# A two-layer decoder step: order of loads and constants at the start, and a last down projection by two token groups

## The chip, the cores and the metric

The kernel runs on one core of one Trainium2 chip. The metric is the device time of one execution in microseconds. The engines named below: PE is the tensor engine (matrix products and transposes, into PSUM), PEld its weight loads, ACT the scalar engine (activation functions, copies, casts), DVE the vector engine, POOL the GpSimd engine, SP the sync engine, which issues most of the transfers. Each engine executes its own queue in order. L12 is line 12 of the kernel before.

## The reference, cut to what matters

One inference step of a decoder of two layers with D_MODEL 1024, for a prompt of 1024 tokens and for 8 sample tokens. Layer 0 mixes by a gated linear recurrence beside attention into 256 memory tokens, layer 1 by stick-breaking attention beside memory attention. Each is followed by a SwiGLU network with 2816 middle columns. What stands at the two ends of the kernel:

```python
def rmsnorm(x, g):
    xf = x.astype(jnp.float32)
    y = xf * lax.rsqrt(jnp.mean(xf * xf, axis=-1, keepdims=True) + EPS)
    return (y * g.astype(jnp.float32)).astype(x.dtype)

def swiglu(h, w_gu, w_down):
    gate, up = jnp.split(h @ w_gu, 2, axis=-1)
    return (jax.nn.silu(gate) * up) @ w_down
...
    for l in range(DEPTH):
        g = g_norm[l]
        hn = rmsnorm(h, g[0])
        if l < N_A:
            mix, S = a_mixer(hn, w_in_a[l], lbs[l], hg_norm[l], mem_k[l], mem_v[l], w_o[l], hg_s0[l])
        else:
            mix = b_mixer(hn, w_in_b[l - N_A], sb_bias[l - N_A], k_all, v_all, q_pos, k_pos, mem_k[l], mem_v[l], w_o[l])
        h = h + rmsnorm(mix, g[1])
        h = h + rmsnorm(swiglu(rmsnorm(h, g[2]), w_gu[l], w_down[l]), g[3])
```

The head of the kernel is the first `rmsnorm` and the product with `w_in_a`; the tail is the last `@ w_down`, its `rmsnorm` and the last sum, for the second half of the prompt and the sample tokens.

## The kernel before, in words

**Layout.** Activations lie with features on the 128 partitions and tokens along the free dimension: a tensor of 1024 features is eight blocks of 128. Tokens go in two groups: group 0 has prompt tokens 0 to 511, group 1 has 512 to 1023 and the 8 sample tokens behind them (520 columns). To keep fp32 accuracy, each operand of a product is split in two fp32r parts, x = hi + lo; a product is three matmuls (w_hi x_hi, w_hi x_lo, w_lo x_hi). A block of weights (four 128x128 tiles, 256 KB) is loaded by SP (L261), cast to its hi part on ACT (L266) and subtracted to its lo part on DVE (L267). Group 1's 520 columns go as two matmuls of 260.

**Order.** The code is written in generators that yield after each piece and are woven together. The kernel language's scheduler then lays out each engine's queue before the run: it goes by the order in which the code issues the instructions, and lets an instruction go ahead of an earlier one where, by its own estimate of times, the earlier one isn't ready yet. It also places the waits and gives out the buffers of a pool (`bufs` of them under one tag). `tc.issue_after(ins)` forces what is issued inside it behind `ins` on that engine.

**Head** (L125 to L216, then `start(0, x0)`, L402). Loads of the norm gains and other parameters into `prow` (L128 to L131), then the four token tiles of group 0 (L134, 128 tokens x 1024 each, 512 KB) on SP. A hint for ACT's table of functions (L135). Constants: the identity, `flip`, `trif`, `bound`, `sel`, and `mask`: for 7 levels and 2 sides two selections on POOL (L169, L173) and a cast to bytes on DVE (L177). `prow` is transposed on PE (L182) into `par`, from which the gains are read. Then the lower bound of the recurrence (L197 to L202), a broadcast of the attention offset (L205, L208) and the page table (L211 to L216). `start(0)` norms the four token tiles: `rms_rows` (L391) takes the sum of squares on ACT (L397, tiles 0 and 2) or on DVE (L395, tiles 1 and 3), Ln and Exp on ACT (L398, L399), and scales the tile on DVE (L400). Then, for each of eight feature blocks, four transposes (L425, one for each tile), the hi part with gain on ACT (L428) and the lo part on DVE (L429). The first product is the value projection `rows_proj` (weights L1074, L1076, L1077; 96 matmuls L1082). `flip` is first read behind it (L1099), the masks in the recurrence (L1285).

**Tail** (class `ffn_w`, L644). The last SwiGLU network, group 1 of layer 1, goes in five parts of 5, 5, 4, 4 and 4 middle tiles. Most middle tiles are computed by `gate_up_w` (L553), which ends with two Silu on ACT (L594, L603), products on DVE and the split of the middle tile (L287, L288). Each part then adds its share of the down projection to R (eight tiles of 128 x 520): for each of eight output blocks m, 24 matmuls of 260 columns (L696), an addition for each half on DVE (L705). In the last part, for each block also the square (L339, L342 on ACT), its accumulation over the blocks (L343 on DVE) and a copy scaled by the norm's gain (L708, ACT). After block 3, `first_half` (L763) transposes blocks 0 to 3 back to token rows. After block 7, `finish_rows` (L776) sums the accumulated squares over the features on PE (L782, L783), takes Ln and Exp on ACT, transposes blocks 4 to 7 (L798), and for each of four row tiles and the sample rows computes row * rstd + residual on DVE in two halves (L799, L802) and stores it (L807, L809). The residual rows were made earlier (`token_rows`, `htok`). L688 is a hint to load ACT's table with both Ln and Exp.

Of the kernel before, what the change touches and what calls it, by code (L numbers as in the profile page):

```python
# [9 lines left out]
F32 = mybir.dt.float32  # L10
F32R = mybir.dt.float32r
# [7 lines left out]
P = 128  # L19
# [5 lines left out]
def tile_decoder(  # L25
# [114 lines left out]
    flip = const.tile([P, P], F32, name="flip")  # L140
    nc.gpsimd.affine_select(
        flip, ones, pattern=[[1, P]], compare_op=ALU.is_equal, fill=0.0, base=1 - P, channel_multiplier=1
    )
    epsb = const.tile([P, 1], F32, name="epsb")
    nc.vector.memset(epsb, EPS)
    trif = const.tile([P, P], F32, name="trif")
    nc.gpsimd.affine_select(
        trif, ones, pattern=[[-1, P]], compare_op=ALU.is_ge, fill=0.0, base=0, channel_multiplier=1
    )
    bound = const.tile([P, P], F32, name="bound")  # L150
    nc.vector.memset(bound, TOP)
    nc.gpsimd.affine_select(
        bound, bound, pattern=[[-1, P]], compare_op=ALU.is_gt, fill=-200.0, base=0, channel_multiplier=1
    )
    sel = const.tile([P, NB, NB], F32, name="sel")
    nc.gpsimd.affine_select(
        sel, ones[:, : NB * NB].rearrange("p (b c) -> p b c", c=NB), pattern=[[1, NB], [-1, NB]],
        compare_op=ALU.is_equal, fill=0.0, base=0, channel_multiplier=0,
    )

    mask = const.tile([P, 7, 2, 64], U8, name="mask")
    for lv in range(7):
        m = 1 << lv
        nb = 64 // m
        for side in range(2):
            o = side * m
# [40 lines left out]
    for blk in range(2):  # L207
        nc.vector.tensor_copy(biass[:, blk], biasp.unsqueeze(2).to_broadcast([P, H, NB]))  # L208
# [1454 lines left out]
```

## Time and profile before

| | us |
|---|---|
| median of 3 runs | 2450.96 (2450.86 to 2453.5) |
| the profiled execution's own time | 2454.44 |
| its span in the trace | 2452.7 |
| PE busy | 2413.9 |
| DVE, ACT, POOL busy | 1563.8, 1204.3, 102.6 |

A busy time of PE is matmuls in flight, not PE at its peak. In a row of the chain of waits stand the start, the length, and what the chain goes through: an instruction of an engine by line, a transfer, or "issue". In a row of the timeline: start, length, engine, line, operation, tiles written and read, count, and in brackets how long the engine was idle before it and who released it. In a row of a single line or tile: count, then the shortest, median and longest duration in ns. q, s and ns are PSUM tiles, ws split weights, w raw weights, m middle tiles, r the tiles R, st the accumulated squares, yT output rows.

### The profile page before, as it was taken

How to read it: one execution, taken by the hardware profiler on the slowest of the kernel's cores; microseconds unless marked ns; L12 is line 12 of the kernel's file. 1: busy time of each engine (PE TensorE's matmuls, PEld its weight loads, DVE VectorE, ACT ScalarE, POOL GpSimd, SP SyncE). 2: the span in 40 equal slices, each digit the busy share in tenths (PEclk: the TensorE clock that was granted, in tenths of full speed). 3: DMA queues.
4: the chain of work that ended last, by engine and by line, in shares of the span. 5: the costliest groups of instructions: out<-in, count | busy, mean ns of one | idle time of the engine just before them, and what ended most of it. 6: DMA issues, size and time to landing. Idle time of an engine off the chain costs nothing.

```text
span 2452.7 us, 40619 instructions
## 1 busy us (share of the span) xinstructions
PE 2413.9 (98%) x15473; PEld 2141.9 (87%) x15473; DVE 1563.8 (64%) x2697; ACT 1204.3 (49%) x2354; POOL 102.6 (4%) x153
## 2 busy tenths in 40 slices
PE   7999999999999999999999999999999999999998
PEld 5888988888877887999999989877787898999997
DVE  5777556765775676555544585677677558655665
ACT  4547544444444454555433454555454445564444
POOL 2000000000000000011111100022000000000000
PEclk9999999999999999999999999999999999999998
DMA  5353252263543446686688866453453244375541
GB/s 177 106 157 104 74 159 84 65 178 118 179 136 95 138 146 210 171 221 150 181 201 220 237 187 189 153 163 118 140 154 117 82 126 125 117 200 148 151 134 66
DMA packets 496726, 360.33 MB, mean 147 GB/s; under 512 B 19181, under 2 KB 443738, under 8 KB 496530
## 3 DMA queue, kind: packets, MB, share of 16 engines
q1 hardware_dynamic: 477970, 303.19, 41.2%
q0 software_dynamic: 18560, 54.53, 9.1%
q8 instruction: 122, 2.00, 0.3%
q14 instruction: 74, 0.61, 0.1%
HBM read 327.83 MB, written 75.96 MB: 165 GB/s over the span
## 4 chain that ended last, share of the span: by engine, by line
PE 90%; DVE 4%; DMA 2%; ACT 2%; issue 1%; SPq 0%; POOL 0%; DVEq 0%; ACTq 0%; POOLq 0%
PE mm L280 62%; PE q L581 7%; PE q L696 5%; PE q L539 2%; PE mm L1082 2%; PE s L932 1%; PE s L891 1%; PE s L1265 1%; PE mm L868 1%; PE s L1440 1%; PE mm L841 1%; DMA b<-qd 1%; PE s L1479 1%; PE s L918 1%; DVE ws L267 1%
## 5 line engine op out<-in xcount | busy, mean ns | idle before, releaser
L280 PE MATMUL mm<-x,ws 128*128 128x260 f32 (+1 forms) x7776 | 1330.4, 330 | 0.0
L280 PEld LDWEIGHTS mm<-x,ws 128*128 128x128 f32 x7776 | 1149.2, 188 | 142.9 <-issue 8.2
L266 ACT CAST ws<-w 128x512 fp32r<-128x512 f32 x712 | 420.1, 591 | 685.7 <-PE mm L280 563.6
L267 DVE TENSOR_TENSOR ws<-w,ws 128x512 fp32r<-128x512 f32 x712 | 462.1, 652 | 263.3 <-ACT ws L266 255.7
L280 PE MATMUL mm<-m,ws 128*128 128x512 f32 (+1 forms) x2112 | 393.1, 343 | 0.4 <-DVE r L476 0.4
L280 PEld LDWEIGHTS mm<-m,ws 128*128 128x128 f32 x2112 | 324.3, 189 | 47.3 <-issue 3.4
L696 PE MATMUL q<-m,ws 128*128 128x260 f32 x1056 | 128.8, 283 | 0.0
L696 PEld LDWEIGHTS q<-m,ws 128*128 128x128 f32 x1056 | 127.2, 188 | 0.4 <-ACT hT L514 0.2
L572 DVE TENSOR_TENSOR ws<-w,ws 128x512 fp32r<-128x512 f32 x126 | 86.5, 691 | 59.7 <-ACT ws L571 57.0
L581 PE MATMUL q<-y,ws 128*128 128x260 f32 x864 | 112.9, 283 | 0.0
L571 ACT CAST ws<-w 128x512 fp32r<-128x512 f32 x126 | 78.0, 621 | 67.9 <-PE q L696 27.4
L581 PEld LDWEIGHTS q<-y,ws 128*128 128x128 f32 x864 | 107.6, 188 | 0.0
L476 DVE TENSOR_TENSOR r<-r,mm 128x512 f32<-128x512 f32 (+1 forms) x96 | 66.0, 687 | 59.9 <-PE mm L280 58.8
L320 DVE TENSOR_SCALAR t<-mm 128x512 f32<-128x512 f32 (+1 forms) x74 | 51.2, 692 | 64.3 <-PE mm L280 64.3
L732 DVE TENSOR_TENSOR t<-t,mm 128x512 f32<-128x512 f32 (+1 forms) x66 | 45.5, 689 | 67.9 <-PE mm L280 67.4
L324 DVE TENSOR_TENSOR t<-t,t 128x512 f32<-128x512 f32 (+1 forms) x66 | 45.8, 694 | 65.7 <-ACT t L323 65.7
L581 PE MATMUL q<-x,ws 128*128 128x260 f32 x648 | 86.3, 282 | 0.0
L581 PEld LDWEIGHTS q<-x,ws 128*128 128x128 f32 x648 | 81.3, 188 | 0.0
L343 DVE TENSOR_TENSOR st<-st,n 128x512 f32<-128x512 f32 (+1 forms) x98 | 67.1, 691 | 6.5 <-ACT n L342 5.0
L287 ACT CAST m<-t 128x512 fp32r<-128x512 f32 (+1 forms) x88 | 54.9, 624 | 25.3 <-DVE t L732 16.5
L1018 POOL DMA_INDIRECT c<-in_cache_sb_k,pidx x16 | 16.4, 1026 | 1128.7 <-issue 919.7
L288 DVE TENSOR_TENSOR m<-t,m 128x512 fp32r<-128x512 f32 (+1 forms) x88 | 60.9, 692 | 2.6 <-ACT m L287 1.4
(356 smaller groups left out, 2513.0 us busy)
## 6 DMA issues: line engine op xcount, KB each, us to landing
w<-in_w_gu SPq DMA_DIRECT2D x334, 256.0 KB, 3.1
w<-in_w_down SPq DMA_DIRECT2D x160, 256.0 KB, 2.7
w<-in_w_in_a SPq DMA_DIRECT2D x80, 256.0 KB, 2.9
wsum<-in_w_gu POOLq DMA_DIRECT2D x18, 1024.0 KB, 8.9
w<-wsum SPq DMA_DIRECT2D x72, 256.0 KB, 3.5
w<-in_w_o SPq DMA_DIRECT2D x64, 256.0 KB, 2.7
wsum<-in_w_gu POOLq DMA_DIRECT2D x12, 1280.0 KB, 10.5
w<-in_w_mem_kv SPq DMA_DIRECT2D x32, 256.0 KB, 3.2
```

The costliest lines, as they stand in the source:

```text
L266: nc.scalar.copy(ws[:, 0, :n, :], raw[:, :n, :])
L267: nc.vector.tensor_sub(ws[:, 1, :n, :], raw[:, :n, :], ws[:, 0, :n, :].bitcast(F32))
L280: nc.tensor.matmul(ps[:, a, : PW[g]], wt, xt[k][:, xi, o : o + PW[g]], start=(k == 0 and wi == 0), stop=(k == nk - 1 and wi == 2),)
L287: nc.scalar.copy(dst[0], src)
L288: nc.vector.tensor_sub(dst[1], src, dst[0].bitcast(F32))
L320: nc.vector.tensor_scalar(sv(x, g), pv(ps, g), -44.0, None, op0=ALU.max)
L343: nc.vector.tensor_add(acc[:, :n], acc[:, :n], t[:, :n])
L476: nc.vector.tensor_add(dst, dst, pv(ps, g))
L571: nc.scalar.copy(w[:, 0, :], src)
L572: nc.vector.tensor_sub(w[:, 1, :], src, w[:, 0, :].bitcast(F32))
L581: nc.tensor.matmul(ps[:, :h], w[:, wj, k * P : (k + 1) * P], x[:, xi, :], start=(first and k == 0 and wi == 0), stop=(k == 3 and wi == 2), ...
L696: nc.tensor.matmul(pp[a][:, :h], wt, mids[k][:, xi, a * h : (a + 1) * h], start=(k == 0 and wi == 0), stop=(k == nf - 1 and wi == 2),)
```

## The change

Two places.

**Head.** The four token tile loads are issued ahead of the four parameter loads, and these go through ACT's queue in place of SP's. `flip`, `trif`, `bound`, `sel`, `mask`, the lower bound, the offsets and the page table are written further down in the code, right before `start(0, x0)`; the code that transposes `prow` stays where it was. The cast of the masks goes from DVE to POOL.

```diff
-    prow = tpool.tile([P, P], F32, tag="t", name="prow")
-    nc.vector.memset(prow, 0.0)
-    nc.sync.dma_start(prow[0:NR, :], g_norm.rearrange("l i (k p) -> (l i k) p", p=P))
-    nc.sync.dma_start(prow[NR : NR + ND, :], g_kv.rearrange("(k p) -> k p", p=P))
-    nc.sync.dma_start(prow[NR + ND : NR + ND + H, :], hg_lb.rearrange("l (h p) -> (l h) p", p=P))
-    nc.sync.dma_start(prow[NR + ND + H : NR + ND + H + 1, :], hg_norm)
     xtok = [rpool.tile([P, CH, D], F32, tag="r", name="xtok0")]
     for tb in range(CH):
         nc.sync.dma_start(xtok[0][:, tb, :], x_prompt[0, tb * P : (tb + 1) * P, :])
+    prow = tpool.tile([P, P], F32, tag="t", name="prow")
+    nc.vector.memset(prow, 0.0)
+    nc.scalar.dma_start(prow[0:NR, :], g_norm.rearrange("l i (k p) -> (l i k) p", p=P))
+    nc.scalar.dma_start(prow[NR : NR + ND, :], g_kv.rearrange("(k p) -> k p", p=P))
+    nc.scalar.dma_start(prow[NR + ND : NR + ND + H, :], hg_lb.rearrange("l (h p) -> (l h) p", p=P))
+    nc.scalar.dma_start(prow[NR + ND + H : NR + ND + H + 1, :], hg_norm)
     nc.scalar.preload_act_table_set("natural_log_exp_and_others")
...
-            nc.vector.tensor_copy(mask[:, lv, side, :], mf.rearrange("p b m -> p (b m)"))
...
+            nc.gpsimd.tensor_copy(mask[:, lv, side, :], mf.rearrange("p b m -> p (b m)"))
```

**Tail.** In the last part of `ffn_w` the down projection goes first over columns 256 to 519 (row tiles 2, 3 and the sample rows), then over 0 to 255 (row tiles 0 and 1). The eight split weights are made once and kept for both; three of them take slots of another pool. Each group has its own sums, norm and row operations; those of the first are issued between the blocks of the second. The square of the last block isn't accumulated on DVE; PE adds it in its sums. `first_half` and `finish_rows` are gone. The table hint is forced behind the last Silu.

```diff
-        nc.scalar.activation(sg[:, h:n], gt[:, :h], AF.Silu)
+        done.append(nc.scalar.activation(sg[:, h:n], gt[:, :h], AF.Silu))
...
             if last:
-                self.acc = small([P, WID], tag="st", bufs=3)
-                nc.scalar.preload_act_table_set("natural_log_exp_and_others")
+                with tc.issue_after(done[-1].ins):
+                    nc.scalar.preload_act_table_set("natural_log_exp_and_others")
+                yield from self.down_rows(mids, f0, nf)
+                return
...
+        def down_rows(self, mids, f0, nf):
+            l, n = self.l, NG[1]
+            hT, hsm = htok[0]
+            acc = small([P, WID], tag="st", bufs=3)
+            yt = [xpool.tile([P, D], F32, tag="x0", name=nm("yT")) for _ in range(CH + 1)]
+            ws = []
+
+            def weight(m):
+                raw = wraw.tile([P, 4, P], F32, tag="w", name=nm("w"))
...
+                if m % 3 == 2 or m == 7:
+                    w = cpool.tile([P, 2, 4, P], F32R, tag="c", name=nm("ws"))
+                else:
+                    w = wspl.tile([P, 2, 4, P], F32R, tag="ws", name=nm("ws"))
+                nc.scalar.copy(w[:, 0], raw)
+                nc.vector.tensor_sub(w[:, 1], raw, w[:, 0].bitcast(F32))
+                return w
+
+            def turned(c, k0):
+                o, w = c * P, (P if c < CH else NB)
+                pt = S()
+                for k in range(4):
+                    nc.tensor.transpose(pt[:w, k * P : (k + 1) * P], self.R[k0 + k][:, o : o + w], ident)
+                return pt[:w]
+
+            def front(cs):
+                for c in cs:
+                    w = P if c < CH else NB
+                    nc.scalar.copy(yt[c][:w, :512], turned(c, 0))
+
+            def stats(cs, sq):
+                ps = NS()
+                r = small([P, 8], tag="rr")
+                for i, c in enumerate(cs):
+                    o, w = c * P, (P if c < CH else NB)
+                    nc.tensor.matmul(ps[:w, i : i + 1], acc[:, o : o + w], ones[:, 0:1], start=True, stop=False)
+                    nc.tensor.matmul(ps[:w, i : i + 1], sq[:, o : o + w], ones[:, 0:1], start=False, stop=True)
...
+                for p, i in parts:
+                    nc.scalar.activation(r[p, i], ps[p, i], AF.Ln, scale=1.0 / D, bias=epsb[p])
+                for p, i in parts:
+                    nc.scalar.activation(r[p, i], r[p, i], AF.Exp, scale=-0.5)
+                return r
+
+            def row(c, rc):
...
+                pt = turned(c, 4)
+                nc.vector.scalar_tensor_tensor(
+                    yt[c][:w, :512], yt[c][:w, :512], rc[:w], h[:w, :512], op0=ALU.mult, op1=ALU.add
+                )
+                nc.vector.scalar_tensor_tensor(
+                    yt[c][:w, 512:], pt, rc[:w], h[:w, 512:], op0=ALU.mult, op1=ALU.add
+                )
...
+            late = []
+            for c0, c1, cs in ((256, n, (2, 3, CH)), (0, 256, (0, 1))):
+                for m in range(ND):
+                    if len(ws) <= m:
+                        ws.append(weight(m))
+                    ps = Q(1 + m % 2)[:, : c1 - c0]
+                    for k in range(nf):
+                        for wi, (wj, xi) in enumerate(((0, 0), (0, 1), (1, 0))):
+                            nc.tensor.matmul(
+                                ps, ws[m][:, wj, k, :], mids[k][:, xi, c0:c1],
+                                start=(k == 0 and wi == 0), stop=(k == nf - 1 and wi == 2),
+                            )
+                    if late:
+                        late.pop(0)()
+                    d = self.R[m][:, c0:c1]
+                    nc.vector.tensor_add(d, d, ps)
+                    if m == 0:
+                        nc.scalar.activation(acc[:, c0:c1], d, AF.Square)
+                    else:
+                        sq = N()
+                        nc.scalar.activation(sq[:, c0:c1], d, AF.Square)
+                        if m < ND - 1:
+                            nc.vector.tensor_add(acc[:, c0:c1], acc[:, c0:c1], sq[:, c0:c1])
+                    nc.scalar.activation(d, d, AF.Copy, scale=gcol(l, 3, m))
+                    if m == 4:
+                        front(cs)
...
+                if c0:
+                    it = rest(cs, sq)
+                    late = [lambda: None] + [lambda: next(it)] * (len(cs) + 1)
+                else:
+                    drain(rest(cs, sq))
...
-    drain(f1.part(2), f1.part(3), f1.part(4), f1.finish_rows())
+    drain(f1.part(2), f1.part(3), f1.part(4))
```

`rest` yields `stats` and then one `row` after the other.

More of the change, by code (lines that the diff above doesn't have):

```diff
@@ L745, in part @@
                 self.now = self.R[m][:, 0:1]
-                if last and self.rows:
-                    nc.scalar.activation(
-                        self.R[m][:, :n], self.R[m][:, :n], AF.Copy, scale=gcol(l, 3, m)
-                    )
-                    if m == 3:
-                        first_half(self)
                 if m % 2:
@@ L1570, in store_y @@
             yield
-    x0, x1 = [], []
+    flip = const.tile([P, P], F32, name="flip")
+    nc.gpsimd.affine_select(
+        flip, ones, pattern=[[1, P]], compare_op=ALU.is_equal, fill=0.0, base=1 - P, channel_multiplier=1
+    )
+    trif = const.tile([P, P], F32, name="trif")
+    nc.gpsimd.affine_select(
+        trif, ones, pattern=[[-1, P]], compare_op=ALU.is_ge, fill=0.0, base=0, channel_multiplier=1
+    )
+    bound = const.tile([P, P], F32, name="bound")
+    nc.vector.memset(bound, TOP)
@@ new lines, in tile_decoder @@
+    lb = const.tile([P, H], F32, name="lb")
+    oml = const.tile([P, H], F32, name="oml")
+    lbt = const.tile([P, H], F32, name="lbt")
+    nc.vector.tensor_sub(lbt, lbraw, lbraw)
+    nc.scalar.activation(lbt, lbt, AF.Exp)
+    nc.vector.reciprocal(lb, lbt)
+    nc.vector.tensor_mul(lbt, lbt, lb)
+    nc.vector.tensor_sub(lb, lbt, lbt)
+    nc.vector.tensor_scalar(oml, lb, -1.0, 1.0, op0=ALU.mult, op1=ALU.add)
+    x0, x1 = [], []
+    biasp = const.tile([P, H], F32, name="biasp")
+    nc.sync.dma_start(biasp, sb_bias.rearrange("o h -> (o h)").partition_broadcast(P))
```

163 lines of the change are left out of this document (54 added, 109 removed).

## The prediction

> **What bounds the kernel now.** I read the page first, then busy time by stretch, then the chain of waits at both ends.
>
> ```profile
> span 2452.7 us, 40619 instructions
> ...
> PE 2413.9 (98%) x15473; PEld 2141.9 (87%) x15473; DVE 1563.8 (64%) x2697; ACT 1204.3 (49%) x2354; POOL 102.6 (4%) x153
> ...
> 0.00:20.00 20.00, 4.71 (x18) 3.11 (x18) 10.71 (x36) 8.28 (x20) 14.12 (x41) 1.00 0.55 199
> ...
> 2400.00:2436.40 36.40, 36.39 (x302) 35.81 (x301) 19.09 (x38) 19.83 (x35) 0.00 (x0) 1.00 0.11 33
> 2436.40:2452.70 16.30, 4.85 (x31) 3.26 (x29) 8.14 (x13) 4.62 (x8) 0.00 (x0) 0.62 0.33 131
> ```
>
> The second to last rows give start and end, length, and the busy time of PE, PEld, DVE, ACT and POOL. PE is idle for 2452.7 - 2413.9 = 38.8 us in all: 15.3 of them in the first 20 us, 11.5 after the last projection, and only 12 in the 2400 us between. The change touches the two ends, and removes no matmul. So it can win at most about 27 us, and what it wins is read from the two end chains. The profiled run took 2454.44 us, 1.74 more than its span and 3.5 above the median of 2450.96; I add the differences in the span to the median.
>
> **The head.** The chain of waits from the first token tile to the first product of the value projection (start, length, what):
>
> ```profile
> 3.03 4.87 DMA xtok<-in_x_prompt
> ...
> 7.92 1.23 DVE c L395
> ...
> 13.88 0.42 DVE mask L177 x2
> 14.30 0.15 DVE lb L201
> 14.46 1.25 DVE c L395
> ...
> 15.76 0.30 ACT rr L398
> ...
> 16.08 0.20 ACT rr L399
> 16.28 1.56 ACT ws L1076 x3
> ...
> 17.88 0.76 DVE xtok L400
> ...
> 18.69 0.49 PE ns L425
> ...
> 19.20 0.70 ACT x L428
> ```
>
> The fourth tile's sum of squares (the second L395) starts at 14.46 although its tile is there earlier. Between the two L395, DVE stands in a queue of mask casts, each waiting for POOL's two selections, and of the small lower-bound operations. The first product starts at 19.20 + 0.70 + 0.04 = 19.94.
>
> When is the tile there? One row gives GB/s in slices of 1 us from 0; the other is the next load of SP that had to wait for a token tile's landing:
>
> ```profile
> GB/s 0 0 262 296 218 320 353 315 328 70 186 392 408 418 344 66 8 0 0 0 127 389 203 115 293 241 340 127 170 174 270 401 342 379 337 280 221 283 267 47
> ...
> 10.51 0.33 SPq L820 DMA_DIRECT2D c<-in_mem_prompt  x1
> ```
>
> Slices 2 to 8 sum to 2.09 MB, which is the four tiles of 512 KB: the bytes were moved by 9.0, and the landing was signalled by about 10.4, 1.4 later. Slice 4 has a dip, because tiles 1 to 3 were issued only from 3.03, behind the four parameter loads.
>
> (1) Token tiles first on SP, the parameter loads on ACT's queue. The four issues come 0.45 apart from 0.80. At the 329 GB/s of slices 5 to 8 the 2.1 MB take 6.4 us from 2.0 to 8.4; with the same 1.4 us the last tile lands at 9.8. Bounds: 8.4 (signalled at once) and 10.4 (nothing won). ACT's four issues, less than the 3.03 us in which SP had issued them and the first tile, lie in its wait for the first tile. The weight loads and the two small broadcasts behind the tiles start earlier; they queue behind the same 2.1 MB.
>
> (2) Mask casts from DVE to POOL. DVE then has, behind the last landing, L395, the scaling L400, and perhaps its lower-bound and bias operations (eight of 0.15 to 0.25 us, about 1.3 in all, of which I charge 0.5 as the rest fits into waits for tiles). From 9.8: + 1.25 (L395) + 0.60 (L398 and L399 with their hops, 15.71 to 16.28) + 0.80 (L400) + 0.55 (PE) + 0.74 (L428) + 0.5 = 14.2. Against 19.94 that is **5.7 us**. The 1.56 us of weight casts in the old chain ran while DVE was late and aren't counted. Bounds: tile at 8.4 and no charge gives 12.3, so 7.6; tile at 10.4, the whole 1.3, and 0.7 for a late parameter transpose gives 16.3, so 3.6. After the first product the phase is as before: eight column blocks by the same ACT, DVE and PE work, then PE without a gap.
>
> (3) POOL's longer queue.
>
> ```profile
> L1285 DVE COPY_PREDICATED b<-mask,s x40: 415/451/805, 113.3 to 463.8; 128x256 f32<-128x256 uint8 x40
> ...
> L173 POOL TENSOR_SCALAR_AFFINE_SELECT mf<-mf x14: 234/290/1477, 3.6 to 17.5; 128x64 f32<-128x64 f32 x14
> ```
>
> The numbers behind the count are shortest, median and longest in ns, then the first and last start. POOL's last selections start at 17.5. A u8 cast on POOL has no row; the nearest is L173 with 0.29 on the same shape. Bounds: 0.21 (DVE's own cast, 0.42 for two above) and 1.48 (L173's longest). At 0.29 the 14 casts add 4 us, at 1.48 20.7: done by 22 to 39, while the masks are first read at 113.3. I count nothing; without that cover it would be those 4 us.
>
> **The tail.**
>
> ```profile
> 2410.65 11.55 PE q L696 x96
> 2422.20 1.31 PE q L768 x12
> ...
> 2424.36 0.66 PE q L768 x4
> ...
> 2425.38 0.59 PE q L773 x4
> 2425.97 10.40 PE q L696 x85
> ...
> 2436.40 0.77 DVE r L705 x2
> ...
> 2437.19 0.65 ACT n L342
> ...
> 2437.86 0.71 DVE st L343
> ...
> 2438.61 1.05 PE q L782 x8
> ...
> 2439.87 1.28 ACT L785
> ...
> 2441.17 0.26 ACT rr L785
> ...
> 2441.58 1.28 ACT L786
> ...
> 2443.12 0.75 DVE yT L799
> ...
> 2449.14 0.66 DVE yTs L802
> ...
> 2449.83 0.30 SPq L809 DMA_DIRECT2D out_y_sample<-yTs  x1
> ```
>
> From PE's last product (2436.38) to the end of the span (2452.70) are 16.32 us: a residual add, square, accumulation, the sums on PE, two loads of activation tables, ten row operations of DVE 0.66 apart, and 2.87 for the last store.
>
> (4) Work moved ahead of the last product. The 192 products stay: 96 of 264 and 96 of 256 columns for 192 of 260, 0.120 each. Ahead of the end stood 20 transposes for 1.31 + 0.66 + 0.59 = 2.56, 0.128 each; now there are 32 (12 halves of the first group in front, 12 behind its norm, 8 of the second group), so + 1.54. The first group's sums are 12 instructions, eight as L782 (1.05) and four narrow ones, between nothing and half of that, of which I take 0.28: + 1.33. PE's last product ends 2.87 later, at 2439.25. All else of the first group (six row operations, 4 us of DVE; its scaled copies on ACT) lies beside the second group's 11.5 us of products; the stretch row shows DVE and ACT busy for 19 to 20 of 36.4 us.
>
> (5) What remains behind the last product: add of half width 0.44, square 0.41 (between half and all of L342's 0.65, as fixed cost stays), no accumulation (PE adds the last square itself), four sum instructions 0.52 + 0.04, Ln 0.06 + 0.26, Exp 0.26, four row operations 0.75 + 3 x 0.66 = 2.73, 0.04, store 2.87: 7.63. Against 16.32 that is 8.69 less.
>
> (6) Table load. The old hint left no load of its own, and Ln and Exp each loaded a set (1.28 twice, 2.56 of the 8.69). Tied behind the last Silu, the hint can only load after it. At the head Ln and Exp follow each other (15.76, 16.08) after one load, so it should hold here. The load falls on ACT's wait before the middle cast:
>
> ```profile
> 2389.11 17.83 SPq L261 DMA_DIRECT2D w<-in_w_down  x8
> ...
> w<-in_w_down SPq DMA_DIRECT2D x160, 256.0 KB, 2.7
> ...
> 2409.24 0.62 ACT L266 CAST ws<-w 128x512 fp32r<-128x512 f32 x1 [1.64 <-PE q L581]
> ...
> 2411.29 0.63 ACT L287 CAST m<-t 128x520 fp32r<-128x520 f32 x1 [1.11 <-DVE t L604]
> 2411.95 0.70 DVE L288 TENSOR_TENSOR m<-t,m 128x520 fp32r<-128x520 f32 x1 [0.69 <-ACT m L287]
> ```
>
> 1.28 less the 1.11 of idle time makes that cast and L288 0.2 late, at 2412.85. They matter more than before: the first output block now reaches its fourth middle tile after 9 products (2411.6), not 18. Bounds: 0 (PE takes products of the next block) and 1.2; I take 0.3.
>
> The Trainium skill (ScalarE: Activation LUTs, What ACT_TABLE_LOAD costs) puts a switch of sets at 2.66 us, half of it a drain. The rows show 1.30 from the load's start to the Ln (2439.87 to 2441.17); by the page the two loads would be worth 5.3 in place of 2.6 and the time would be 2.7 lower. The measurement decides.
>
> (7) Weights at twice the rate. A block of weights is now needed each 1.45 us, not 2.9, and all eight stay until the end. The eight loads were issued by 2406.94, and the fifth cast ran at 2409.24, before the first product; the three more are 1.9 us of ACT. ACT in the first group: 1.9 + 1.28 + 0.63 + 8 x (0.41 for the square + 0.41 for the scaled copy) + 3 copies at the cast's 0.62 = 12.2 against 11.55 + 12 x 0.128 = 13.1 of PE. That is close, but a late copy stops only transposes. Bounds: 0, and 2.0 if only two blocks are ready early. I take 0.
>
> Tail: 8.69 - 2.87 - 0.3 = **5.5 us**, between 3.5 and 6.7 (the added transposes at 0.108, nothing of (6)).
>
> **Sum.** 5.7 + 5.5 = 11.2: span 2441.5, and 2450.96 - 11.2 = 2439.8 us. The bounds together give 7.1 to 14.3, thus 2436.7 to 2443.9; 1.5 more each way for the stretch between, whose order on each engine shifts.
>
> **Rivals.** A: parameters late. The four small loads now run beside 2.1 MB; if they land with the last tile, DVE's in-order queue holds the second L395 behind the lower-bound operations (transpose and copy 0.8, then 1.2): 10.4 + 2.0 + 1.25 + 0.6 + 0.8 + 0.55 + 0.74 = 16.3, a gain of 3.6 and 2441.9. For it: 14.30, where such an operation stands in the chain ahead of L395. Against: the tile loads leave ACT's queue free from the start.
>
> B: the change doesn't do what it says with the table: the hint is again without a load, both loads come back behind the last product: + 2.56, 2442.4. For it: the old hint left no row. Against: the order after the Silu is now forced.
>
> C: POOL holds DVE. L173's longest, 1.48 for a median of 0.29, lies beside the first L395, so the two engines do hold each other up; L395 itself took 1.23 and 1.25, so here it was POOL that waited. If POOL's longer queue held DVE for one whole selection at each of the four L400 and the eight weight subtractions of the value projection, that were 12 x 0.29 = 3.5 of the head's gain: 2443.3. The Trainium skill (SBUF — State Buffer, Who interferes with whom) says that whichever of the two starts first holds the pair for its whole instruction, and names an operation with two SBUF inputs such as these subtractions; the trace bears out the holding, in the other direction.
>
> D: nothing comes of it. Both ends shrink, but PE's idle time in the middle rises by what they gave, because all queues are laid out anew: about 2450. For it: 12 us of idle time in the middle show that the order matters. Against: they are spread over 2400 us, and the stages are PE's.
>
> E, slower: the doubled rate of weights in the first token group. If loads aren't ahead, each block waits for a slot, then load 2.7 (the row above, issue to landing), cast 0.62, subtraction about 0.7, 4.0 us in line: 8 x (4.0 - 1.45) = 20.4 lost against 11.2 won, 2460. It makes the whole slower from (11.2 + 4.9) / 8 + 1.45 = 3.5 us a block. For it: five load buffers, slots held to the end. Against: all eight loads were issued 3.5 us before the first product, and three blocks get slots of another pool.
>
> **Chances.** The forecast 0.60, A 0.10, B 0.10, C 0.05, D 0.09, E 0.06. About 0.2%, 4.9 us, is what a measurement of this kernel can tell from no change, so faster means under 2446.1: the forecast, A, B and C nearly whole, 0.84; same 0.10; slower 0.06. The likeliest's own range is 2435.2 to 2445.4, which holds A to C; I take 2435 to 2446.
>
> **What would show it.** The first L1082 product near 14.2 (12.3 to 16.3) and no mask cast on DVE. One table load after the last L603 and none behind the last product. PE's last product 2.9 later than before relative to the start of the last down projection, the span's end 7.6 behind it, four row operations between. PE without gaps of over 1 us between the blocks of the first group. If the first product starts after 17, or the weights' casts end each of PE's waits there, the forecast is wrong in that step; if both ends are as said and the time isn't, the middle took it (D).

## The result, and the profile after

The changed kernel takes 2442.05 us (median of 6 runs, 2438.43 to 2443.04) where the kernel before takes 2451.31 beside it (6 runs, 2450.86 to 2453.5): a ratio of 0.9956 [0.9947, 0.9966], faster by 9.3 us. A second set of runs gave 2440.78 against 2452.09, 0.9955 [0.9942, 0.9969]. The forecast was 2439.8, its range 2435 to 2446.

The page of the changed kernel's profile, span and engines:

```profile
span 2439.7 us, 40660 instructions
...
PE 2410.5 (99%) x15483; PEld 2140.8 (88%) x15483; DVE 1561.0 (64%) x2688; ACT 1205.8 (49%) x2371; POOL 106.3 (4%) x167
```

PE is idle for 2439.7 - 2410.5 = 29.2 us, 9.6 less than before, with the same products; the rest of the 13.0 by which the two spans differ is busy time of PE. Where the idle time lies, by stretch (start and end, length, busy time of PE, PEld, DVE, ACT and POOL, then the clock granted to PE as a share of full speed, the busy share of the DMA engines, and GB/s):

```profile
0.00:20.00 20.00, 10.88 (x47) 8.34 (x48) 13.25 (x30) 12.43 (x27) 16.08 (x42) 1.00 0.82 268
100.00:120.00 20.00, 17.88 (x115) 16.05 (x114) 14.69 (x30) 6.82 (x15) 0.00 (x0) 0.91 0.50 145
2430.00:2439.70 9.70, 2.76 (x23) 2.32 (x21) 3.58 (x6) 2.19 (x6) 0.00 (x0) 0.78 0.27 108
```

PE's busy time in the first 20 us rose from 4.71 to 10.88, so 6.2 of the gain stand there. The last row shows 6.9 us without PE at the end, where 11.5 were before. The middle row has 2.1 us of idle time between 100 and 120 us and a granted clock of 0.91; the experiments come to both.

**The head after.** The chain of waits of the changed kernel from the fourth token tile on:

```profile
2.42 6.88 DMA xtok<-in_x_prompt
...
9.43 0.42 DVE c L335
...
10.58 0.08 DVE rr L335
10.66 0.10 DVE lbt L1594
10.77 0.24 DVE biass L1607 x2
11.01 0.60 DVE xtok L340
...
11.66 0.48 PE ns L365
12.13 0.64 PE s L365 x3
...
13.02 0.70 ACT x L368
...
13.76 1.89 PE mm L1064 x4
```

L335, L340, L365, L368 and L1064 are the old L395, L400, L425, L428 and L1082. The tile lands at 9.30 and DVE begins 0.13 later; no mask cast and no selection stands in the chain. The first product starts at 13.76 instead of 19.94.

**The tail after.** The chain of the same kernel in the last down projection:

```profile
2410.39 1.31 PE q L675 x12
...
2426.54 4.27 PE q L722 x36
...
2430.89 0.35 PE q L688 x2
2431.25 0.71 PE q L675 x6
2431.96 0.18 PE q L689 x2
2432.14 0.22 PE q L688 x2
...
2432.68 0.27 ACT rr L693
...
2433.21 0.75 DVE yT L702
```

L722 are the products of the down projection, L675 the transposes to rows, L688 the sums over the accumulated squares and L689 those over the last block's squares. Behind the last product (2430.81) no table load is left; Ln and Exp follow the sums directly. But six transposes of the row tiles stand between the sums.

The timeline of the changed kernel shows the only table load, the last cast of the down weights, the one stop of PE, and the last store:

```profile
2402.29 1.28 ACT L628 ACT_TABLE_LOAD   x1
2404.12 0.62 ACT L667 CAST ws<-w 128x512 fp32r<-128x512 f32 x1
2404.26 0.92 PEld L722 LDWEIGHTS q<-m,ws 128*128 128x128 f32 x7 [0.27 <-ACT m L227]
2435.98 0.33 SPq L710 DMA_DIRECT2D out_y_prompt<-yT  x1
```

### The profile page after: what moved, and what is told of

Same layout as the page of the kernel before. It is cut to its first block, busy times and chain, and to the rows that moved or that the text cites. A ratio compares the mean times of both kernels' runs of the same rounds, so it can differ in the third digit from the quotient of the medians.

```text
span 2439.7 us, 40660 instructions
## 1 busy us (share of the span) xinstructions
PE 2410.5 (99%) x15483; PEld 2140.8 (88%) x15483; DVE 1561.0 (64%) x2688; ACT 1205.8 (49%) x2371; POOL 106.3 (4%) x167
## 4 chain that ended last, share of the span: by engine, by line
PE 92%; DVE 3%; DMA 2%; ACT 1%; issue 1%; SPq 0%; DVEq 0%; ACTq 0%; POOLq 0%; POOL 0%
PE mm L220 63%; PE q L521 7%; PE q L638 4%; PE q L479 2%; PE mm L1064 2%; PE s L914 1%; PE s L873 1%; PE s L1422 1%; PE s L1247 1%; PE mm L850 1%; PE q L722 1%; PE s L1461 1%; PE mm L823 1%; PE s L900 1%; DMA b<-qd 1%
## 5 line engine op out<-in xcount | busy, mean ns | idle before, releaser
L206 ACT CAST ws<-w 128x512 fp32r<-128x512 f32 x704 | 414.8, 590 | 674.0 <-PE mm L220 556.4
L207 DVE TENSOR_TENSOR ws<-w,ws 128x512 fp32r<-128x512 f32 x704 | 456.6, 652 | 259.9 <-ACT ws L206 254.8
L512 DVE TENSOR_TENSOR ws<-w,ws 128x512 fp32r<-128x512 f32 x126 | 86.5, 691 | 59.7 <-ACT ws L511 57.0
L511 ACT CAST ws<-w 128x512 fp32r<-128x512 f32 x126 | 78.0, 621 | 68.2 <-PE q L638 27.3
L638 PE MATMUL q<-m,ws 128*128 128x260 f32 x864 | 104.7, 282 | 0.0
L638 PEld LDWEIGHTS q<-m,ws 128*128 128x128 f32 x864 | 103.8, 188 | 0.3 <-ACT hT L454 0.2
L283 DVE TENSOR_TENSOR st<-st,n 128x512 f32<-128x512 f32 (+1 forms) x91 | 62.2, 691 | 3.1 <-ACT n L282 1.5
```

The source lines that it names most:

```text
L206: nc.scalar.copy(ws[:, 0, :n, :], raw[:, :n, :])
L207: nc.vector.tensor_sub(ws[:, 1, :n, :], raw[:, :n, :], ws[:, 0, :n, :].bitcast(F32))
L283: nc.vector.tensor_add(acc[:, :n], acc[:, :n], t[:, :n])
L511: nc.scalar.copy(w[:, 0, :], src)
L512: nc.vector.tensor_sub(w[:, 1, :], src, w[:, 0, :].bitcast(F32))
L638: nc.tensor.matmul(pp[a][:, :h], wt, mids[k][:, xi, a * h : (a + 1) * h], start=(k == 0 and wi == 0), stop=(k == nf - 1 and wi == 2),)
```

## The experiments

The kernels below are compared by two measures: the time against runs of the kernel before on the same chip, and, in their traces, the start of one and the same cast of split weights on ACT. How much earlier it starts than in the first profile of before is a kernel's lead at that place. These are its rows in the timelines of before and after, for the place at 70 us, where the value projection is through:

```profile
70.52 0.62 ACT L266 CAST ws<-w 128x512 fp32r<-128x512 f32 x1
```

```profile
63.19 0.62 ACT L206 CAST ws<-w 128x512 fp32r<-128x512 f32 x1
```

The difference is a lead of 7.33. The leads of all profiles (us), beside the start of the first product of the value projection:

| kernel | first product | lead at 70 | at 125 | at 1809 | at 2399 |
|---|---|---|---|---|---|
| before | 19.94 | 0 | 0 | 0 | 0 |
| before_again | 19.07 | 1.69 | 1.73 | 3.03 | 3.31 |
| tail_alone | 19.72 | 0.68 | -0.83 | -0.85 | 1.35 |
| tail_again | 19.29 | 0.81 | -0.39 | 1.14 | 1.44 |
| casts_on_dve | 18.13 | 2.02 | 1.26 | 3.40 | 5.25 |
| after | 13.76 | 7.33 | 4.07 | 5.37 | 7.91 |
| both_again | 14.11 | 5.96 | 4.77 | 7.91 | 10.40 |
| head_alone | 14.41 | 6.02 | 4.72 | 5.50 | 7.32 |
| casts_alone | 14.39 | 6.36 | 4.92 | 6.35 | 8.25 |
| loads_back | 14.83 | 6.23 | 5.67 | 9.99 | 11.85 |
| hint_free | 13.90 | 7.09 | 5.92 | 7.90 | 10.51 |
| sums_halves | 14.70 | 6.35 | 5.33 | 7.86 | 7.96 |
| tok_other_pool | 14.31 | 4.96 | 5.58 | 7.39 | 7.85 |
| best | 14.82 | 5.20 | 5.84 | 9.00 | 9.03 |

Two executions of one kernel (before and before_again) differ by 1.7 us at 70 and by 3.3 at 2399. So single profiles can't settle a question of 2 us behind the head; means over several, and the times, can.

**1. Which end gives what.** both_again is the changed kernel unchanged.

> The changed kernel a second time. Theory: the head's 7.3 us shrink to 4.1 in the stage of the memory keys (about 100 to 115 us), where PE waits for the store out_mk_prompt, and the tail gives 5.0: 9.1 us less than before in every profile, apart from a varying 2 to 3 us near 1840 us (a load b<-qd). Rival: that loss was chance in one profile; then this profile shows the casts of the split weights behind 120 us 7.3 us earlier than before, and the time is about 12 us below.

2440.78 us, 0.9955 [0.9942, 0.9969]: 11.3 less than the 2452.09 beside it. Neither side of the expectation fits: from 70 to 125 us this profile loses 1.2, not 3.2 and not nothing (experiment 4).

head_alone is the kernel before with the change's head:

```diff
+    xtok = [rpool.tile([P, CH, D], F32, tag="r", name="xtok0")]
...
+    nc.scalar.dma_start(prow[0:NR, :], g_norm.rearrange("l i (k p) -> (l i k) p", p=P))
...
+            nc.gpsimd.tensor_copy(mask[:, lv, side, :], mf.rearrange("p b m -> p (b m)"))
```

> The head of the change with the old tail. Theory: value projection done 7.3 us earlier, 3.2 of it lost at the memory keys, so 4.1 us faster in all, about 2447.2. Rival (nothing is lost): 7.3 faster, 2444.

2444.08 us, 0.9967 [0.9954, 0.9979]: 8.0 less than the runs of before beside it; the interval makes that 5.1 to 11.3. The forecast's 5.7 lies inside, the expected 4.1 doesn't; the rival's 7.3 is nearer. The trace is the finer measure at the head itself: the nine profiles with POOL's casts (two of them, casts_alone and loads_back below, have the old order of the loads) start the first product at 14.36 on average, the four with the old head at 19.50, and lead at 70 us by 6.2 and 0.8. That is 5.1 and 5.4 us.

tail_alone is the kernel before with the change's tail:

```diff
-        nc.scalar.activation(sg[:, h:n], gt[:, :h], AF.Silu)
+        done.append(nc.scalar.activation(sg[:, h:n], gt[:, :h], AF.Silu))
...
+                with tc.issue_after(done[-1].ins):
+                    nc.scalar.preload_act_table_set("natural_log_exp_and_others")
+                yield from self.down_rows(mids, f0, nf)
+                return
...
-    drain(f1.part(2), f1.part(3), f1.part(4), f1.finish_rows())
+    drain(f1.part(2), f1.part(3), f1.part(4))
```

> The tail of the change with the old head. Theory: 42.2 us from the first product of the last down projection to the end become 37.2: 5.0 us faster, about 2446.3, and the head's chain is as before (first L1082 product at 19.9). Rival: the tail only works out when the head's order also changed: no gain.

2447.72 us, 0.9981 [0.9972, 0.999]: 4.4 less. Here too the trace is finer: from the first product of the last down projection to the end the four profiles with the old tail (before, before_again, head_alone, casts_alone) take 42.2 to 42.3 us, the seven with the change's tail as it stands (after, both_again, tail_alone, tail_again, casts_on_dve, loads_back, tok_other_pool) 37.1 to 37.2. So the tail gives 5.1. By the times, the two parts sum to 12.4 and the whole gave 9.3 and 11.3: by these intervals they add up, and neither takes from the other.

**2. Which edit of the head.** The head has three: the order of the loads, the casts' engine, and the place of the constants in the code. casts_on_dve is the changed kernel with the casts back:

```diff
-            nc.gpsimd.tensor_copy(mask[:, lv, side, :], mf.rearrange("p b m -> p (b m)"))
+            nc.vector.tensor_copy(mask[:, lv, side, :], mf.rearrange("p b m -> p (b m)"))
```

> The changed kernel with the mask casts back on DVE; load order and place in the code stay. Theory (the casts in DVE's queue were what held the second sum of squares): first product at 18 to 20, value projection done 4 to 6 us later than with the change, and the time 0 to 5 us above it, as the loss at the memory keys takes part of any shift. Rival (the load order made the gain): first product at 14, no difference.

2447.49 us, 0.9982 [0.9973, 0.9991]: 6.7 of the 11.3 us are gone, more than the 5 that the theory allowed; 3.9 of them stand between the two leads at 70 us. The end of its chain of waits in the head:

```profile
15.52 0.41 DVE mask L1589 x2
...
16.08 0.75 DVE xtok L340
...
18.13 2.08 PE mm L1064 x4
```

Two mask casts, the last of a row that waited for POOL's selections, stand again ahead of the scaling of the last tile, although the code now has the constants behind the loads. Of the head's 5.4 us at 70 us, the lead of 2.02 less the 0.8 of the old head leaves 1.2. casts_alone is the reverse, the kernel before with nothing but the casts on POOL:

```diff
-            nc.vector.tensor_copy(mask[:, lv, side, :], mf.rearrange("p b m -> p (b m)"))
+            nc.gpsimd.tensor_copy(mask[:, lv, side, :], mf.rearrange("p b m -> p (b m)"))
```

> The kernel before with one edit: the mask casts on POOL. Theory (the casts are the whole gain of the head, the load order and the places in the code give nothing that shows): first product at 13.5 to 15.5, time 5 to 8 us below the kernel before, as the head alone gave 8.0. Rival (the old load order or the old place of the constants costs its own 1 to 2 us): 4 to 6 below.

2446.27 us, 0.9977 [0.9968, 0.9986]: 5.5 less than before, where head_alone had 8.0; the intervals overlap. Its chain of waits:

```profile
10.18 1.12 DVE c L395
...
14.39 2.08 PE mm L1082 x4
```

The last sum of squares starts at 10.18 where it started at 14.46, with the loads in their old order; the first product comes at 14.39, as in head_alone (14.41). loads_back is the changed kernel with the loads in their old order:

```diff
+    nc.sync.dma_start(prow[0:NR, :], g_norm.rearrange("l i (k p) -> (l i k) p", p=P))
...
     xtok = [rpool.tile([P, CH, D], F32, tag="r", name="xtok0")]
...
-    nc.scalar.dma_start(prow[0:NR, :], g_norm.rearrange("l i (k p) -> (l i k) p", p=P))
```

> The changed kernel with the old order of loads: parameters first, all on SP; the mask casts stay on POOL. Theory (the casts made most of the head's gain, the load order about 1 us): the last token tile's wait ends at 10.4 in place of 9.3 to 9.9, first product at 14.6 to 15.4, time 0.5 to 1.5 us above the changed kernel. Rival (both parts are needed, and each alone gives about 1 us, as casts back on DVE left 1.3 of the head's gain): first product at 18, time 6 us above.

2442.95 us against 2452.84, 0.9958 [0.9945, 0.9972]: 9.9 less, between the 9.3 and the 11.3 of the two sets with the new order. Its chain of waits:

```profile
5.97 7.57 DMA w<-in_w_in_a
13.57 0.62 ACT ws L1058
...
14.83 1.91 PE mm L1064 x4
```

Here the first weights come last: their load lands at 13.54, and their cast stands ahead of L368 on ACT. The first product is 0.5 later than the mean of the others and the lead at 70 us (6.23) is theirs. The order of the loads is worth nothing that can be seen behind the value projection, where two profiles of one kernel differ by 1.7. The casts are what can be seen of the head's gain.

**3. The tail's terms.** hint_free is the changed kernel with the table hint no longer tied to the last Silu:

```diff
-                with tc.issue_after(done[-1].ins):
+                if True:
                     nc.scalar.preload_act_table_set("natural_log_exp_and_others")
```

> The changed kernel with the table hint not tied behind the last Silu. Theory: the hint leaves no load, as before the change; Ln and Exp of each token group load their sets, 4 loads in the tail; the two of the second group stand in the last chain, 2.56 us more, those of the first don't count; from the last product to the end 11.4 us in place of 8.9. Rival: the tail's order keeps the table loaded and nothing changes.

2443.49 us, 0.9963 [0.995, 0.9977]: 9.4 less than before, where the changed kernel had 9.3 and 11.3, so the times don't show what the tie is worth. The trace does; its chain of waits in the tail:

```profile
2417.29 1.28 ACT L693
...
2419.00 1.28 ACT L695
...
2431.58 1.28 ACT L693
...
2432.88 0.26 ACT rr L693
...
2433.16 1.28 ACT L695
```

Without the tie there are four loads, two for each token group. The last product ends at about 2429.7, the span at 2441.2: 11.5 us, where the changed kernel has 2439.7 - 2430.81 = 8.9. The last two loads cost 2.6, their own length: the Ln starts 1.30 behind its load, as in the kernel before. The Trainium skill (ScalarE: Activation LUTs, What ACT_TABLE_LOAD costs) has 2.66 us for one switch, half of it a drain. Here the drain isn't seen; an estimate from that figure, taken twice, would have made the difference 5.3.

The loads of the first group were expected not to count, but they stand in the chain too: ACT's and DVE's work for the next blocks comes late, and PE stands idle for 1.32 us before a transpose at 2425.30. From the first product of the last down projection to the last one it takes 29.7 us for 28.2. From that first product to the end it is 41.2 for 37.1, so the tie is worth 4.1 us in the trace.

sums_halves puts the sums over the accumulated squares of both row tiles ahead of those over the last squares, and stores each half of a row tile as soon as it is made:

```diff
-                for i, c in enumerate(cs):
-                    o, w = c * P, (P if c < CH else NB)
-                    nc.tensor.matmul(ps[:w, i : i + 1], acc[:, o : o + w], ones[:, 0:1], start=True, stop=False)
-                    nc.tensor.matmul(ps[:w, i : i + 1], sq[:, o : o + w], ones[:, 0:1], start=False, stop=True)
+                for first, t in ((True, acc), (False, sq)):
+                    for i, c in enumerate(cs):
+                        o, w = c * P, (P if c < CH else NB)
+                        nc.tensor.matmul(
+                            ps[:w, i : i + 1], t[:, o : o + w], ones[:, 0:1], start=first, stop=not first,
...
+                if c < CH:
+                    nc.sync.dma_start(y_prompt[0, t0 : t0 + P, :512], yt[c][:, :512])
...
-                    nc.sync.dma_start(y_prompt[0, t0 : t0 + P, :], yt[c])
+                    nc.sync.dma_start(y_prompt[0, t0 : t0 + P, 512:], yt[c][:, 512:])
```

In this kernel the sums of squares of the output rows are incomplete: the second column's sum is opened in the same PSUM bank before the first column's is ended. The work is the same.

> The changed kernel with two edits at the very end: the accumulated squares of all row tiles are summed ahead of the last block's squares, and each output row tile is stored in two halves as they are ready. Theory (what my forecast of the tail's end missed are PE's sums, 0.85 us behind the last square for 0.52, and the last store, 3.75 us from issue to the end for 2.87): last product to the end 8.9 becomes 8.0 (0.35 by the sums, 0.6 by a last store of half the size). Rival: the end after the last store is fixed and two more stores cost issue time: 8.6 to 9.2.

2441.25 us, 0.9956 [0.9943, 0.997]. From the last product (2430.91) to the end (2439.4) it takes 8.5 us, 0.4 less than the changed kernel. The theory's 8.0 is missed. The transposes still stood between the sums, and the first sum over the last squares now started 0.2 behind its square instead of 0.05; so the reordering gave next to nothing (the Ln starts 1.8 behind the last product, 1.9 before it), and the half stores gave 0.3. The time can't tell 0.4.

**4. What was lost between 70 and 125 us.** The changed kernel's lead falls there from 7.33 to 4.07, by 3.26. Its chain of waits has a store in it:

```profile
103.14 5.93 DMA out_mk_prompt<-t
```

The transposed memory keys go out from the buffer `t`, whose slot ACT's next copy (L828) needs; PE waits for that copy. In the kernel before the same row is

```profile
110.47 4.22 DMA out_mk_prompt<-t
```

PE's rows behind that copy, in before, after and both_again in turn:

```profile
115.21 0.44 PE L849 MATMUL mm<-ident,t 128*128 128x128 f32 x2 [0.42 <-ACT t L846]
```

```profile
109.59 0.44 PE L831 MATMUL mm<-ident,t 128*128 128x128 f32 x2 [2.12 <-ACT t L828]
...
110.01 7.36 PE L220 MATMUL mm<-x,ws 128*128 128x512 f32 x24
```

```profile
110.86 5.80 PE L220 MATMUL mm<-x,ws 128*128 128x512 f32 x24
```

So the loss has two parts. The wait for the store is 2.12 us for 0.42, 1.7 more. The other 1.6 is the clock: in this one profile PE got half its clock from 110.9 to 114.3 us (the 0.91 of the stretch row), and the same 24 products took 7.36 us, where they took 5.80 in the other execution of this kernel and in before. Only the first part comes back in every profile with an edit and the old buffer: PE waits there for 1.0 to 2.1 us, 0.4 in both executions of before.

I first took the longer store for the change's doing: the head leaves other transfers beside it. Two runs were to tell that from chance. before_again is the kernel before once more, tail_again is tail_alone once more, which has the old head.

> The kernel before once more, for a second profile. Theory (the loss of 3.2 us at the memory keys was chance in the first profile of before, whose store landed after 4.2 us, not a cost of the changed head): the store out_mk_prompt lands after 5 to 6 us here too, the casts of weights behind 120 us come 0.5 to 2 us later than in the first profile. Rival: 4.2 again.

2451.14 us; the store took 4.19, as the rival said.

> The old head with the new tail once more, for a second profile of the stage of the memory keys. If the landing of out_mk_prompt there is chance from run to run, it lies anywhere between 4.2 and 5.9 us; if it belongs to the kernel (two profiles of before gave 4.2 both times), it is near the 5.75 of this kernel's first profile.

2447.88 us. With the old head, the store took 5.42 here and 5.75 in tail_alone. So the head isn't its cause: the kernel with the old head and the new tail, whose code differs only 2300 us later, loses 1.5 and 1.2 us there too. Chance doesn't explain it well either: it took 4.22 and 4.19 in the two executions of before, and 4.79 to 5.93 in all twelve executions of kernels with an edit. It isn't this store alone: the 256 KB load of weights that SP issued 0.4 us ahead of it landed after 3.4 us in before and 6.0 in after. What makes them longer stays open. That PE waits for it can be undone: tok_other_pool is the changed kernel with that buffer in another pool.

```diff
-            tok = T()
+            tok = N()
             nc.vector.tensor_copy(tok[:, :NM], pt[:, :NM])
```

> The changed kernel with the token rows of the memory keys in another pool (2 buffers that lie idle there) in place of the three-buffer pool that also holds the keys. Theory: the wait for the store out_mk_prompt at 104 to 110 us (2.6 and 2.4 us on ACT, in every profile, with the old head too) is a buffer freed late; with it gone PE gets 2 to 4 us there, and it varies less. Rival: the wait moves to the store of the other tile (mks), gain under 1 us.

2437.76 us, 0.9939 [0.9926, 0.9953]: 15.1 less than before, where the changed kernel had 9.3 and 11.3; the intervals overlap. PE's row at this place:

```profile
109.69 0.38 PE L831 MATMUL mm<-ident,t 128*128 128x128 f32 x2
```

PE no longer waits there, and no store is in the chain, though this store took 4.84. In the seven other profiles with POOL's casts and the old buffer (after, both_again, head_alone, casts_alone, loads_back, hint_free, sums_halves) PE waits there for 1.0 to 2.1 us, 1.6 on average. That is what the other buffer is worth in the traces; the larger gain in the time isn't explained.

**5. All that the runs pointed to.** best is the changed kernel with that buffer in the other pool, and in the last row group the two sums in PSUM banks of their own, the accumulated squares first, the transposes forced behind the sums, and the rows stored in halves:

```diff
+                tail = CH not in cs
+                one = None if tail else NS()
+                ps = [NS()[:, 0:1] if tail else one[:, i : i + 1] for i in range(len(cs))]
...
+                    for t in (acc, sq):
+                        for i in range(len(cs)):
+                            end = add(i, t, t is acc)
+                    ends.append(end)
...
+                    with tc.issue_after(ends[0].ins):
+                        pt = turned(c, 4)
...
+                    nc.sync.dma_start(y_prompt[0, t0 : t0 + P, :512], yt[c][:, :512])
...
-            tok = T()
+            tok = N()
```

> The changed kernel with the token rows of the memory keys in the other pool, the last two row tiles' sums in two PSUM banks with the accumulated squares first, the transposes of blocks 4 to 7 of these tiles forced behind the sums, and output rows stored in halves. Theory: from the last product to the end 8.9 becomes 7.7 (0.7 by the six transposes that stood between the sums, 0.4 by the last store), the memory keys give 2 to 3 us: 2437 to 2438. Rival: the transposes, now late, hold the second half of each row on DVE and the end stays at 8.5.

2436.12 us against 2451.79 beside it, 0.9933 [0.9919, 0.9946]: 15.7 less than the kernel before, and the lowest median of the study. Its chain of waits at the end:

```profile
2429.73 0.43 DVE r L749
...
2430.19 0.42 ACT n L754
...
2430.64 0.46 ACT r L757
...
2431.14 0.43 ACT rr L706 x2
```

From the last product (2429.71) to the end (2437.9) it takes 8.2 us instead of 8.9. PE is out of the chain; instead ACT's copy scaled by the gain (L757) stands between the square and the Ln. The end is shorter by 0.7, where 1.2 were expected: the Ln starts 1.4 behind the last product instead of 1.9, and the last store takes 3.45 to the end for 3.75. The other buffer's 1.6 of experiment 4 comes on top: 2.3 by the traces, where the gains of best and both_again, each against the runs beside it, differ by 4.4 and their intervals just overlap.

## Why the prediction was right, point by point

**The head's 5.7 was 5.1 to 5.4,** and its mechanism is shown from both sides: casts_alone has the gain in the trace without the rest of the head, casts_on_dve lacks most of it with all the rest. Part (1) put the order of the loads at 0.6; the fourth tile did land 0.5 earlier than that (9.30 for 9.8), yet nothing of it can be told in loads_back at 70 us. From landing to first product the forecast had 4.4 and the trace has 13.76 - 9.30 = 4.5, and the sum of part (2) comes out term by term: the scaling 0.83 for 0.80, the transposes 0.58 for 0.55, the copy 0.74 for 0.74. But one term has its size by luck. Between the fourth tile's sum of squares and its scaling the forecast had 0.60 for Ln and Exp and 0.5 for small operations, 1.1; it took 1.0, and the timeline shows with what:

```profile
9.68 0.20 ACT L339 ACTIVATE rr<-rr 128x1 f32<-128x1 f32 x1
10.86 0.74 DVE L340 TENSOR_SCALAR xtok<-xtok,rr 128x1024 f32<-128x1024 f32 x1
11.02 0.20 ACT L339 ACTIVATE rr<-rr 128x1 f32<-128x1 f32 x1
11.61 0.83 DVE L340 TENSOR_SCALAR xtok<-xtok,rr 128x1024 f32<-128x1024 f32 x1
```

The first L340 is the third tile's. Its Exp had ended at 9.88, but DVE's queue had the fourth tile's sum ahead of it (9.43 to 10.66). So the third tile's scaling came behind that sum, and the fourth's, whose Exp had ended at 11.23, waited for it until 11.61. The small operations took 0.34 of the chain. The forecast has the third tile's scaling nowhere behind the last landing.

**Part (3), POOL's longer queue, cost nothing.** The rows of the mask tile, in the changed kernel:

```profile
L1267 DVE COPY_PREDICATED b<-mask,s x40: 417/436/807, 105.9 to 459.7; 128x256 f32<-128x256 uint8 x40
L1589 POOL CAST mask<-mf x14: 226/231/681, 8.6 to 22.2; 128x64 uint8<-128x64 f32 x14
```

The last cast starts at 22.2, the lower end of the forecast's 22 to 39, and the first read is at 105.9. The casts take 0.23, a little less than the 0.29 charged.

**The tail's 5.5 was 5.1 by the traces** (first product of the last down projection to the end, experiment 1) and 4.4 by the time of tail_alone, inside 3.5 to 6.7. Two terms were off, in opposite directions, so the sum is nearer than its terms by luck.

- Part (4) put the last product 2.87 later, and (6) 0.3 more. From the first product to the last it took 28.2 us (2402.58 to 2430.79), 2.2 longer than before (26.0). The transposes are 0.109 each (1.31 for 12), not the 0.128 that the old rows gave with their mixed counts, which makes the 32 cost 0.94 more than the old 20, not 1.54; the first group's sums took 0.96 (2418.93 to 2419.89), not 1.33. PE waited 0.27 for the middle tile's cast behind the table load, as (6) had it.
- Part (5) gave 7.63 from the last product to the end; 8.9 were measured. The Ln starts 1.87 behind the last product instead of 1.41. The six transposes held nothing up here: the first sum over the last squares started 0.05 behind its square. But the code adds column by column, so the second column's accumulated squares (2432.14 above) stand behind the first column's last squares. Six sum instructions were left behind the square where the forecast counted four, and from the square's end to the Ln it took 0.98 for 0.56. In best, with four left and a bank for each column, it took 0.53. And the store of a whole row tile took 3.75 from its issue (2435.98) to the end, where the forecast took 2.87 from the sample rows' store of 32 KB. Ln, Exp and the four row operations were as forecast (2432.68 to 2435.95).

Parts (6) and (7): one table load behind the last Silu, none behind the last product. The last of the eight weight casts starts at 2404.12, 1.5 us after that first product; PE waited for none of them.

**The rivals.** A (parameters late) didn't come: the lower-bound operations stand in the chain with 0.34 in all, not 2.0. B is what hint_free shows: behind the last product it is the forecast's 2.56 when the tie is taken away, and 1.5 more ahead of it, so the tie is what held. C (POOL holds DVE) isn't seen: POOL's selection stretched again, to 1.50, beside DVE's sum of squares, which took 1.22. The four L340 took 3.3 us together, where the four L400 had taken 3.0, and the weight subtractions 0.67 to 0.72 each, as before (0.68 to 0.69): nothing near 3.5. D has a grain: the middle moves by some us from one execution to the next (leads at 2399 from 7.3 to 11.9 with POOL's casts, from 0 to 3.3 with the old head), more than the 1.5 the forecast allowed, but not against the change: on average the difference grew from 5.4 at 70 us to 7.5 at 2399. Part of that is the clock. Both executions of before have two stretches of 3.4 us at half the granted clock (from 945.4 and 1843.1, and from 942.8 and 1840.5), four profiles (tail_again, sums_halves, tok_other_pool, best) have one near 1840, after has the one at 110.9, and the other seven have none until PE's last products are done. The four profiles with the old head have 1.25 of them on average, the nine with POOL's casts 0.44; at the 1.6 us of experiment 4 that is, as an estimate, 1.3 of the 2.1. E didn't come. That the two profiles' spans differ by 13.0 and the medians by 9.3 and 11.3 is no term of its own: the profiled run of before lay 3.5 above its median, and the forecast had taken its differences from rows and put them on the median.

## What to carry to other kernels

An in-order queue with small operations that each wait for another engine delays whatever large operation stands behind them: look at what the engine waits for in the gap, and move the small ones to the engine they wait for. An edit that moves loads earlier is worth only what the next latecomer leaves; here it couldn't be told. Take the price of a last store from a store of its own size. Pin a table hint by an explicit order. Write the last sums in the order in which their operands come, and force other work behind them, as best does. Before you give a few us to an edit, look at the granted clock of both profiles in that stretch.

## What the runs showed of the hardware

One and the same store of memory keys took 4.2 us in both executions of one kernel and 4.8 to 5.9 in others which differ from it elsewhere. A last store of 512 KB took 3.75 us from issue to the end of the span, one of 256 KB 3.45 (best, issued at 2434.45, end 2437.9), one of 32 KB 2.87: of it, little goes with the size. PE can lose half its clock for 3.4 us in the middle of the kernel: after had such a stretch from 110.9, 1.3 us after a wait of PE of 2.12 ended, and the same 24 products took 7.36 us for 5.80; both_again had none after a wait of 1.62 at the same place, tail_alone none after one of 1.96.
